# Last attention steps of a group laid over the next projection, embedding products in value banks, squares read from the bank

## Chip, core and metric

The kernel runs on one core of a Trainium2 chip. Its time is the device time of one execution in microseconds (us); lower is better. The core's engines are TensorE (PE, matmuls and transposes), VectorE (DVE), ScalarE (ACT), GpSimd (POOL) and SyncE (SP, which issues the DMAs here). Each engine runs its own instructions in order and waits for others by semaphores. Matmul results land in PSUM, which holds eight banks of 128 x 512 f32.

## What is computed

A decoder trunk of two layers, 512 tokens, width 1024. Layer 0 mixes tokens by eight stick-breaking heads and four differential heads, layer 1 by sixteen dilated heads. After each mixer come a squared-ReLU MLP and a gated per-layer embedding. The parts that matter:

```
h = h + even_mixer(hn, ...)          # layer 0;  odd_mixer in layer 1
  proj = h @ w_in;  q, k, v = split(proj)
  stick-breaking: w = sigmoid(z) * prod of later (1 - sigmoid(z)),  o = w @ v
  differential:   attn = softmax(s0) - lam * softmax(s1),  o = rmsnorm(attn @ v, subln_g) * (1 - lambda_init)
  return concat(o) @ w_out
u = square(relu(hn @ w_mlp_up));  h = h + u @ w_mlp_down
h = h + (p @ w_ple_proj) * sigmoid(rmsnorm(h) @ w_ple_gate)     # embedding products: p @ w_ple_proj
```

## The kernel before, in words

All products are made from f32 numbers split into a high and a low part (a copy on ACT, a subtraction on DVE or POOL), three matmuls each (`mm3`, lines 138, 141 and 142). Weights come in blocks by DMA and are split by `wsplit` (L122 on ACT, L126 on POOL).

A mixer has four groups of heads. In layer 0 these are two differential groups (two heads each), then two stick-breaking ones (four heads each); in layer 1 four dilated ones. `project(g)` makes the values, queries and keys of a group, 96 units of PE work in the order of the generator. `attend(...)` gives the group's steps as a list. Step n forms the scores and weights of tile n (head n // 4, query tile n % 4). It also transposes tile n - 3 and copies it into `pth` and `ptl` (L540, L541), and `combine(x)` multiplies the four tiles of a head by the values, five steps after the head's last tile. In differential groups `subnorm(x)` comes two steps later: it squares the head's output, sums over the partitions by two matmuls with `ones_r` (L622, L623) and scales by the inverse root (`rsqrt`: Ln on L210, Exp on L213, DVE on L214 to L216). Dilated and stick-breaking groups have 21 steps, differential ones 15.

`interleave(units, total, steps)` lays the steps of group n between the units of group n + 1's projection, evenly, after a lead of 8 units. All steps of a group lie within that one projection. The last group of layer 0 lies over `ple_units(1)` and `out_first`, that of layer 1 over `out_first`. The embedding products of layer 0 (`ple_units(0)`, eight of them in 512 columns) stand ahead of the last projection of the mixer, the first of them after the last differential group's steps. Each takes a bank of the pool "mm", is copied out by ACT (L365) into a tile (`tmp2` or `pjt`) and stored to DRAM.

PSUM pools have two banks each: "mm" for projections, "sc" for scores, "tp" for transposes, "pv" for combines and sub-norm sums. A bank is free again when its reader is done. `tmp2` has three buffers, which the sub-norms and the embedding products share.

The instructions' order on each engine comes from the tile framework's scheduler, which takes the program's order and the dependencies. It need not be the written order.

The built program has an instruction ACT_TABLE_LOAD on ACT wherever Sigmoid (the stick-breaking scores, L590 and L591) follows Ln or Exp (norms and softmax), and the other way round; copies and Squares stand anywhere without one.

Of the kernel before, what the change touches and what calls it, by code (L numbers as in the profile page):

```python
# [12 lines left out]
F32 = mybir.dt.float32  # L13
F32R = mybir.dt.float32r
I32 = mybir.dt.int32
AF = mybir.ActivationFunctionType
ALU = mybir.AluOpType
# [6 lines left out]
QT = S // P  # L24
# [10 lines left out]
PVLAG = 2  # L35
# [27 lines left out]
def trunk(  # L63
# [5 lines left out]
    nc = tc.nc  # L69
    uid = [0]  # L70

    def nm(s):
        uid[0] += 1
        return f"{s}_{uid[0]}"
# [15 lines left out]
    def t2k(tag, pool=None, dtype=F32):  # L90
        return (pool or (mix[0] if tag in ("tmp", "tmp2") else spool)).tile([P, S], dtype, tag=tag, name=nm(tag), bufs=T_BUFS.get(tag, 2))
# [6 lines left out]
    def ps(tag):  # L98
        return psum.tile([P, S], F32, tag=tag, name=nm(tag), bufs=PS_BUFS[tag])
# [4 lines left out]
    def ps_wide():  # L104
        t = ps(wide[wide_i[0] % 8])
        wide_i[0] += 1
        return t
# [4 lines left out]
    def wload(src):  # L112
        raw = wpool.tile([P, src.shape[-1]], F32, tag="raw", name=nm("raw"), bufs=2)
        nc.sync.dma_start(raw, src)
        return raw
# [41 lines left out]
    def run(units):  # L157
        for _ in units:
            pass

    LEAD = 8.0

    def interleave(units, total, steps):
        spent, at = -LEAD, 0
        for cost in units:
            spent += cost
            while at < len(steps) and at * (total - LEAD) < spent * len(steps):
                steps[at]()
                at += 1
        for step in steps[at:]:  # L170
            step()

    last_split = []
# [174 lines left out]
    def ple_units(layer):  # L348
        raw = wpool.tile([P, 2 * KT * P], F32, tag="raw", name=nm("raw"), bufs=2)
        nc.sync.dma_start(raw[:, 0:2 * S].rearrange("p (k c) -> p k c", k=2), pT[layer].rearrange("k p c -> p k c"))  # L350
        ph, pl = wsplit(raw, 0, 2, S)
        raw = wload(w_proj[layer])
        for c in range(2):
            wh, wl = wsplit(raw, c, 2, 512)
            for i in range(4):
                acc = ps("mm")
                sl = slice(i * P, (i + 1) * P)
                for k in range(2):
                    if layer < DEPTH - 1:
                        mm3(acc, wh[:, k, sl], wl[:, k, sl], ph[:, k], pl[:, k], k == 0, k == 1)  # L360
                    else:
                        mm3(acc, ph[:, k, sl], pl[:, k, sl], wh[:, k], wl[:, k], k == 0, k == 1)
                    yield 2.0
                t = mix[0].tile([P, S], F32, tag="bias", name=nm("pjt"), bufs=4) if i % 2 else t2k("tmp2")
                nc.scalar.activation(t, acc, AF.Copy)  # L365
                nc.sync.dma_start(pjd[layer, 4 * c + i], t)
# [5 lines left out]
    def mixer(layer, norm, nxt):  # L372
# [182 lines left out]
        def attend(g, kind, v, heads):  # L555
            LAG = 3
            nh = 2 if kind == "diff" else 4
            pts = [(pt_i[0] + x) % 2 for x in range(nh)]
            pt_i[0] += nh
            bias, ready = {}, {}  # L560

            def weights(x, i, evict):
                n = P * (i + 1)
# [34 lines left out]
            def combine(x):  # L598
                hi, lo = pth[pts[x]], ptl[pts[x]]
                if kind == "diff":  # L600
                    vh = lambda j: v[:, j, P * x:P * x + P]
                    vl = lambda j: v[:, j, 256 + P * x:256 + P * x + P]
                    op = pv([(vh, hi), (vh, lo), (vl, hi)])
                    o = oT[2 * g + x]
                    nc.scalar.activation(o, op, AF.Copy)
                    return
                vs = lambda j: v[:, j, P * x:P * x + P]
                op = pv([(vs, hi), (vs, lo)])
                a = slice(64 * (x % 2), 64 * (x % 2) + 64)
                b = slice(64 - 64 * (x % 2), 128 - 64 * (x % 2))  # L610
                o = oT[2 * g + x // 2]
                nc.scalar.activation(o[a], op[b], AF.Copy)
                nc.vector.tensor_tensor(o[a], op[a], o[a], op=ALU.add)

            def subnorm(x):
                o = oT[2 * g + x]
                hi, rs, lo = t2k("tmp2", dtype=F32R), t2k("tmp2"), t2k("tmp2", dtype=F32R)
                nc.scalar.activation(rs, o, AF.Square)
                nc.scalar.activation(hi, rs, AF.Copy)
                nc.vector.tensor_tensor(lo, rs, hi.bitcast(F32), op=ALU.subtract)  # L620
                mp = ps("pv")
                nc.tensor.matmul(mp, ones_r, hi, start=True, stop=False)  # L622
                nc.tensor.matmul(mp, ones_r, lo, start=False, stop=True)  # L623
                rsqrt(rs, t2k("tmp2"), mp, SUBLN_EPS, eps_s, scale=float(D // P))
                nc.vector.scalar_tensor_tensor(o, o, gsub, rs, op0=ALU.mult, op1=ALU.mult)

            def step(n):
                m = n - LAG
                evict = lambda: None
                if 0 <= m < QT * nh:  # L630
                    tp = transpose(ready.pop(m), m % QT)
                    evict = lambda: transposed(tp, m % QT, pts[m // QT])
                if n < QT * nh:
                    ready[n] = weights(n // QT, n % QT, evict)
                else:
                    evict()
                m = n - LAG - PVLAG
                if m >= 0 and m % QT == QT - 1 and m // QT < nh:
                    combine(m // QT)
                m -= 2  # L640
                if kind == "diff" and m >= 0 and m % QT == QT - 1 and m // QT < nh:
                    subnorm(m // QT)

            return [(lambda n=n: step(n)) for n in range(QT * nh + LAG + PVLAG + 2 * (kind == "diff"))]

        groups = GROUPS[layer]
        tiles = [2 * g + d for g in groups for d in range(2)]
# [2 lines left out]
        def spread(units, every):  # L650
            for x, cost in enumerate(units):
                if x % every == 0 and len(ohl) < 6:
                    ohl.append(split_tile(oT[tiles[len(ohl)]]))
                yield cost
# [13 lines left out]

        cur = []
        run(project(groups[0], cur))  # L670
        for n, g in enumerate(groups[1:]):
            steps = attend(*cur)
            cur = []
            if layer == 0 and n == 2:
                interleave(chain(ple_units(0), project(g, cur)), 132.0, steps)
            else:
                interleave(project(g, cur), 100.0, steps)
        if layer == 0:
            interleave(chain(spread(ple_units(1), 2), out_first()), 100.0, attend(*cur))
        else:  # L680
            interleave(out_first(), 72.0, attend(*cur))
        ohl += [split_tile(oT[k]) for k in tiles[6:8]]
        for c, (wh, wl) in enumerate(block(w_outb[layer], 2, 512)):
            for i in range(4):
                acc = ps_wide()
# [344 lines left out]
```

## Time and profile before

| what | value |
|---|---|
| median of the runs | 1310.36 us (1309.34 to 1310.42) |
| profiled execution | 1308.87 us |
| its span, first to last instruction | 1307.1 us |
| busy: PE / DVE / ACT / POOL | 1283.7 / 973.5 / 686.0 / 189.8 us |
| layer 0's mixer | about 0 to 262 us |
| layer 1's mixer | about 684 to 890 us |

The times of engines overlap, so the busy times don't add up to the span. A row of the page or of a view names a line of the kernel (L122), the engine, the tiles written and read (`wh<-raw`), and then the times. An idle time in brackets is the engine's, right before the instruction, with what released it.

### The profile page before, as it was taken

The numbers are of one execution on the slowest core, as the hardware profiler recorded it, in microseconds if no ns is written. First come the engines' busy times: TensorE is split into PE (matmuls) and PEld (weight loads), VectorE is DVE, ScalarE is ACT, GpSimd is POOL, SyncE is SP. The second block draws the span as 40 slices with busy tenths as digits, with TensorE's granted clock in tenths as the row PEclk, the third lists the DMA queues.
The fourth block names the chain that finished last, engine by engine and source line by source line (L and its number), as shares of the span: only waits on it lengthen the run. The fifth ranks groups of instructions, "written<-read, shape, count | busy, mean of one in ns | idle before, by whom it ended". The sixth has DMA issues, their size and how long they took to land.

```text
span 1307.1 us, 18561 instructions
## 1 busy us (share of the span) xinstructions
PE 1283.7 (98%) x7256; PEld 1117.4 (85%) x7256; DVE 973.5 (74%) x1623; ACT 686.0 (52%) x1117; POOL 189.8 (15%) x160
## 2 busy tenths in 40 slices
PE   9999999999999999999999999999999999999997
PEld 7988787888998989988889888788899898998876
DVE  7788888778848869845767877887784885994566
ACT  6666768554535334333456666765553443533344
POOL 2433434410000000000024333222000000000001
PEclk9999999999999999999999999999999999999999
DMA  6421423223232322323432222212223123232241
GB/s 217 135 81 50 140 93 115 89 82 112 86 108 97 102 92 97 129 97 101 157 112 96 84 89 78 69 57 95 99 97 124 70 97 129 73 122 97 97 145 65
DMA packets 28040, 133.20 MB, mean 102 GB/s; under 512 B 3312, under 2 KB 4048, under 8 KB 15280
## 3 DMA queue, kind: packets, MB, share of 16 engines
q1 hardware_dynamic: 27952, 132.01, 29.5%
q8 instruction: 57, 0.93, 0.3%
q14 instruction: 31, 0.25, 0.1%
HBM read 125.63 MB, written 6.37 MB: 101 GB/s over the span
## 4 chain that ended last, share of the span: by engine, by line
PE 85%; DVE 8%; ACT 4%; issue 1%; DMA 1%; SPq 0%; POOL 0%; ACTq 0%; DVEq 0%; POOLq 0%
PE mm L138 10%; PE mm L141 10%; PE mm L142 10%; PE sc L141 6%; PE sc L142 6%; PE sc L138 6%; PE pv L142 5%; PE pv L141 5%; PE pv L138 5%; PE tp L141 5%; PE tp L142 5%; PE tp L138 5%; PE pv L551 2%; PE tp L532 2%; PE sc L506 1%
## 5 line engine op out<-in xcount | busy, mean ns | idle before, releaser
L122 ACT ACTIVATE wh<-raw 128x1024 fp32r<-128x1024 f32 (+1 forms) x168 | 173.4, 1036 | 226.9 <-PE mm L141 63.0
L126 POOL TENSOR_TENSOR wl<-raw,wh 128x512 fp32r<-128x512 f32 (+1 forms) x132 | 177.1, 1364 | 309.3 <-ACT wh L122 303.6
L138 PE MATMUL mm<-hi,wh 128*128 128x512 f32 x472 | 187.0, 396 | 0.6 <-DVE v L443 0.4
L142 PE MATMUL mm<-hi,wl 128*128 128x512 f32 x472 | 184.8, 392 | 0.1
L141 PE MATMUL mm<-lo,wh 128*128 128x512 f32 x472 | 184.6, 391 | 0.0
L128 DVE TENSOR_TENSOR wl<-raw,wh 128x1024 fp32r<-128x1024 f32 x102 | 124.5, 1224 | 41.3 <-ACT wh L122 34.8
L142 PEld LDWEIGHTS mm<-hi,wl 128*128 128x128 f32 x472 | 88.6, 188 | 20.1 <-POOL wl L126 0.5
L138 PEld LDWEIGHTS mm<-hi,wh 128*128 128x128 f32 x472 | 88.7, 188 | 17.3 <-DVE v L443 0.6
L141 PEld LDWEIGHTS mm<-lo,wh 128*128 128x128 f32 x472 | 88.7, 188 | 15.6
L526 ACT ACTIVATE e<-e,mn 128x128 f32<-128x128 f32 (+3 forms) x96 | 53.8, 561 | 65.4 <-DVE mn L523 65.0
L754 ACT ACTIVATE wh<-raw 128x1024 fp32r<-128x1024 f32 x48 | 50.7, 1057 | 69.6 <-PE tp L141 35.1
L733 DVE TENSOR_TENSOR ul<-u,uh 128x1792 fp32r<-128x1792 f32 (+1 forms) x32 | 58.4, 1824 | 23.4 <-ACT uh L732 23.4
L732 ACT ACTIVATE uh<-u 128x1792 fp32r<-128x1792 f32 (+1 forms) x32 | 49.4, 1544 | 48.9 <-DVE u L728 48.7
L138 PE MATMUL sc<-hi,wh 128*128 128x512 f32 x184 | 71.9, 391 | 0.9 <-ACT hi L182 0.9
L141 PE MATMUL sc<-lo,wh 128*128 128x512 f32 x184 | 72.1, 392 | 0.3 <-DVE lo L183 0.3
L142 PE MATMUL sc<-hi,wl 128*128 128x512 f32 x184 | 71.8, 390 | 0.0
L721 ACT ACTIVATE u<-u 128x512 f32<-128x512 f32 x64 | 39.4, 625 | 53.8 <-DVE u L720 53.8
L142 PE MATMUL pv<-uh,wl 128*128 128x256 f32 (+1 forms) x224 | 67.4, 301 | 0.0
L142 PE MATMUL sc<-uh,wl 128*128 128x256 f32 (+1 forms) x224 | 67.3, 301 | 0.0
L141 PE MATMUL pv<-ul,wh 128*128 128x256 f32 (+1 forms) x224 | 67.2, 300 | 0.0
L141 PE MATMUL sc<-ul,wh 128*128 128x256 f32 (+1 forms) x224 | 67.2, 300 | 0.0
L138 PE MATMUL pv<-uh,wh 128*128 128x256 f32 (+1 forms) x224 | 66.6, 297 | 0.0
(259 smaller groups left out, 3645.4 us busy)
## 6 DMA issues: line engine op xcount, KB each, us to landing
raw<-in_w_up_dram SPq DMA_DIRECT2D x32, 1024.0 KB, 4.9
raw<-in_w_down_dram SPq DMA_DIRECT2D x32, 1024.0 KB, 4.9
raw<-in_w_in_dram SPq DMA_DIRECT2D x23, 1024.0 KB, 4.9
raw<-in_w_gate_dram SPq DMA_DIRECT2D x8, 1024.0 KB, 5.0
bias<-urow SPq DMA_DIRECT2D x24, 256.0 KB, 3.9
raw<-in_w_outa_dram SPq DMA_DIRECT2D x8, 768.0 KB, 4.2
pj<-pjd SPq DMA_DIRECT2D x16, 256.0 KB, 5.0
h<-in_xT_dram SPq DMA_DIRECT2D x8, 256.0 KB, 5.6
```

Of the source, the lines that this page charges most:

```text
L122: nc.scalar.activation(hi, src, AF.Copy)
L126: nc.gpsimd.tensor_tensor(lo[:, kx], src[:, kx], hi[:, kx].bitcast(F32), op=ALU.subtract)
L128: nc.vector.tensor_tensor(lo, src, hi.bitcast(F32), op=ALU.subtract)
L138: mm = nc.tensor.matmul(acc, lh, rh, start=start, stop=False)
L141: nc.tensor.matmul(acc, lh, rl, start=False, stop=False)
L142: nc.tensor.matmul(acc, ll, rh, start=False, stop=stop)
L526: nc.scalar.activation(e[:, 0:n], e[:, 0:n], AF.Exp, scale=-1.0, bias=mn, accum_out=s)
L532: nc.tensor.transpose(tp[:, j * P:(j + 1) * P], e[:, j * P:(j + 1) * P], ident)
L721: nc.scalar.activation(ui, ui, AF.Square, scale=0.5)
L732: nc.scalar.activation(uh[:, parts], u[:, parts], AF.Copy)
L733: nc.vector.tensor_tensor(ul[:, parts], u[:, parts], uh[:, parts].bitcast(F32), op=ALU.subtract)
L754: nc.scalar.activation(hi, src, AF.Copy)
```

## The change

Three edits.

1. `attend` gives two lists: the main steps (the first 4 x heads + 1, that is 17 or 9), and those left, in which only late transposes, the last combine and (in differential groups) both sub-norms happen. `interleave` takes the left ones of the group before as `tail` and lays them evenly into the first ten units (`LEAD` is 10.0, it was 8.0); the main steps follow, evenly over the other units. The last group of a layer gets its left steps behind its main ones.
2. Two of the eight embedding products, numbers 2 and 5, take a bank of "pv"; the others keep "mm".
3. Both Squares of the sub-norm (`hi` rounded, `rs` in full) are made by ACT straight from the product's bank at combine, with the copy to `o`; DVE's difference `lo` follows there. They are held until `subnorm` uses them. Before, both were made at `subnorm`, from `o`.

```diff
--- before.py
+++ after.py
@@ -158,16 +158,18 @@
         for _ in units:
             pass
 
-    LEAD = 8.0
-
-    def interleave(units, total, steps):
-        spent, at = -LEAD, 0
+    LEAD = 10.0
+
+    def interleave(units, total, steps, tail=()):
+
+        plan = [(LEAD * (x + 1) / (len(tail) + 1), step) for x, step in enumerate(tail)]
+        plan += [(LEAD + x * (total - LEAD) / len(steps), step) for x, step in enumerate(steps)]
+        spent = 0.0
         for cost in units:
             spent += cost
-            while at < len(steps) and at * (total - LEAD) < spent * len(steps):
-                steps[at]()
-                at += 1
-        for step in steps[at:]:
+            while plan and plan[0][0] < spent:
+                plan.pop(0)[1]()
+        for _, step in plan:
             step()
 
     last_split = []
@@ -353,7 +355,7 @@
         for c in range(2):
             wh, wl = wsplit(raw, c, 2, 512)
             for i in range(4):
-                acc = ps("mm")
+                acc = ps("pv" if (4 * c + i) % 3 == 2 else "mm")
                 sl = slice(i * P, (i + 1) * P)
                 for k in range(2):
                     if layer < DEPTH - 1:
@@ -557,7 +559,7 @@
             nh = 2 if kind == "diff" else 4
             pts = [(pt_i[0] + x) % 2 for x in range(nh)]
             pt_i[0] += nh
-            bias, ready = {}, {}
+            bias, ready, squares = {}, {}, {}
 
             def weights(x, i, evict):
                 n = P * (i + 1)
@@ -602,7 +604,12 @@
                     vl = lambda j: v[:, j, 256 + P * x:256 + P * x + P]
                     op = pv([(vh, hi), (vh, lo), (vl, hi)])
                     o = oT[2 * g + x]
+                    hi, rs, lo = t2k("tmp2", dtype=F32R), t2k("tmp2"), t2k("tmp2", dtype=F32R)
+                    nc.scalar.activation(rs, op, AF.Square)
+                    nc.scalar.activation(hi, op, AF.Square)
                     nc.scalar.activation(o, op, AF.Copy)
+                    nc.vector.tensor_tensor(lo, rs, hi.bitcast(F32), op=ALU.subtract)
+                    squares[x] = (rs, hi, lo)
                     return
                 vs = lambda j: v[:, j, P * x:P * x + P]
                 op = pv([(vs, hi), (vs, lo)])
@@ -614,10 +621,7 @@
 
             def subnorm(x):
                 o = oT[2 * g + x]
-                hi, rs, lo = t2k("tmp2", dtype=F32R), t2k("tmp2"), t2k("tmp2", dtype=F32R)
-                nc.scalar.activation(rs, o, AF.Square)
-                nc.scalar.activation(hi, rs, AF.Copy)
-                nc.vector.tensor_tensor(lo, rs, hi.bitcast(F32), op=ALU.subtract)
+                rs, hi, lo = squares.pop(x)
                 mp = ps("pv")
                 nc.tensor.matmul(mp, ones_r, hi, start=True, stop=False)
                 nc.tensor.matmul(mp, ones_r, lo, start=False, stop=True)
@@ -641,7 +645,8 @@
                 if kind == "diff" and m >= 0 and m % QT == QT - 1 and m // QT < nh:
                     subnorm(m // QT)
 
-            return [(lambda n=n: step(n)) for n in range(QT * nh + LAG + PVLAG + 2 * (kind == "diff"))]
+            steps = [(lambda n=n: step(n)) for n in range(QT * nh + LAG + PVLAG + 2 * (kind == "diff"))]
+            return steps[:QT * nh + 1], steps[QT * nh + 1:]
 
         groups = GROUPS[layer]
         tiles = [2 * g + d for g in groups for d in range(2)]
@@ -668,17 +673,20 @@
 
         cur = []
         run(project(groups[0], cur))
+        tail = ()
         for n, g in enumerate(groups[1:]):
-            steps = attend(*cur)
+            steps, left = attend(*cur)
             cur = []
             if layer == 0 and n == 2:
-                interleave(chain(ple_units(0), project(g, cur)), 132.0, steps)
+                interleave(chain(ple_units(0), project(g, cur)), 132.0, steps, tail)
             else:
-                interleave(project(g, cur), 100.0, steps)
+                interleave(project(g, cur), 100.0, steps, tail)
+            tail = left
+        steps, left = attend(*cur)
         if layer == 0:
-            interleave(chain(spread(ple_units(1), 2), out_first()), 100.0, attend(*cur))
+            interleave(chain(spread(ple_units(1), 2), out_first()), 100.0, steps + left, tail)
         else:
-            interleave(out_first(), 72.0, attend(*cur))
+            interleave(out_first(), 72.0, steps + left, tail)
         ohl += [split_tile(oT[k]) for k in tiles[6:8]]
         for c, (wh, wl) in enumerate(block(w_outb[layer], 2, 512)):
             for i in range(4):
```

Below, the order of the built programs, engine by engine, at the places where the prediction speaks of them. The numbers in names count buffers; they differ between the two programs.

ACT at the end of the second differential group, before: the embedding products are copied out on L365, `e` are the sigmoids, `tmp2_328` is the last sub-norm's.

```order
L122 ACTIVATE wh_355_1706<-raw_338_1639 128x1024
L213 ACTIVATE tmp2_328_1604<-tmp2_328_1604 128x512
L488 ACTIVATE kh_333_1624<-tmp_332_1622 64x512
L489 ACTIVATE kh_333_1624<-tmp_332_1622 64x512
L488 ACTIVATE kh_334_1628<-tmp_332_1622 64x512
L489 ACTIVATE kh_334_1628<-tmp_332_1622 64x512
L365 ACTIVATE tmp2_342_1653<-mm_341_1646 128x512
L365 ACTIVATE pjt_344_1663<-mm_343_1656 128x512
L590 ACT_TABLE_LOAD
L590 ACTIVATE e_347_1674<-sc_346_1670 128x128
L591 ACTIVATE e_348_1675<-sc_346_1670 128x128
```

The last sub-norm's Exp (L213) stands ahead of all sigmoids, with one table load between them. After, in the same stretch, `tmp2_340` is the last sub-norm's (Ln on L212, Exp on L215), and nine rows ahead of the first one stands another load:

```order
L367 ACTIVATE pjt_351_1693<-mm_350_1686 128x512
L122 ACTIVATE wh_376_1780<-raw_373_1776 128x1024
L212 ACT_TABLE_LOAD
L212 ACTIVATE tmp2_340_1644<-pv_344_1660,eps_s_83 128x512
L592 ACT_TABLE_LOAD
L592 ACTIVATE e_363_1739<-sc_362_1735 128x384
L215 ACT_TABLE_LOAD
L215 ACTIVATE tmp2_340_1644<-tmp2_340_1644 128x512
L593 ACT_TABLE_LOAD
L593 ACTIVATE e_364_1740<-sc_362_1735 128x384
L367 ACTIVATE tmp2_349_1683<-pv_343_1656 128x512
```

Ln and Exp now stand between the sigmoids of the first stick-breaking head, and each change between them has a load: five in this stretch, where there was one.

PE, before, where embedding product 2 begins (`mm_345`), after the scores of a stick-breaking tile:

```order
L506 MATMUL sc_351_1690<-kh_324_1560,qq_293_1411 128x256
L507 MATMUL sc_351_1690<-klz_25_183,qq_293_1411 128x256
L509 MATMUL sc_351_1690<-sbmask_90,ident_r_92 128x128
L138 MATMUL mm_345_1666<-wh_336_1634,wh_339_1641 128x512
L141 MATMUL mm_345_1666<-wl_337_1635,wh_339_1641 128x512
L142 MATMUL mm_345_1666<-wh_336_1634,wl_340_1642 128x512
L138 MATMUL mm_345_1666<-wh_336_1634,wh_339_1641 128x512
```

After, where product 5 begins (`pv_359`), in the bank that the last sub-norm's sum (`pv_344`) held:

```order
L138 MATMUL mm_361_1731<-wh_326_1581,wh_352_1696 128x512
L141 MATMUL mm_361_1731<-wl_327_1582,wh_352_1696 128x512
L142 MATMUL mm_361_1731<-wh_326_1581,wl_353_1697 128x512
L534 MATMUL tp_367_1758<-ident_72,e_347_1677 128x128
L508 MATMUL sc_368_1762<-kh_306_1489,qq_264_1332 128x512
L509 MATMUL sc_368_1762<-klz_25_183,qq_264_1332 128x512
L511 MATMUL sc_368_1762<-sbmask_90,ident_r_92 128x128
L534 MATMUL tp_378_1806<-ident_72,e_356_1709 128x128 x2
L138 MATMUL pv_359_1721<-wh_326_1581,wh_352_1696 128x512
L141 MATMUL pv_359_1721<-wl_327_1582,wh_352_1696 128x512
L142 MATMUL pv_359_1721<-wh_326_1581,wl_353_1697 128x512
```

Product 2 moved to a "pv" bank too (`pv_343`), ahead of this stretch; product 5 waits for DVE's read of `pv_344` (L217 of the new file), where before each product waited for the copies of those in the two "mm" banks.

PE in layer 1, at the end of the third dilated group's steps, before: `mm_1538` is the last key tile of the projection, `pv_1564` the last combine.

```order
L142 MATMUL mm_1538_8263<-hi_1091_6294,wl_1536_8258 128x512
L138 MATMUL mm_1538_8263<-hi_1095_6306,wh_1535_8257 128x512
L141 MATMUL mm_1538_8263<-lo_1096_6307,wh_1535_8257 128x512
L142 MATMUL mm_1538_8263<-hi_1095_6306,wl_1536_8258 128x512
L551 MATMUL pv_1564_8401<-pth_1103_6326,v_1292_7232 128x512
L551 MATMUL pv_1564_8401<-ptl_1105_6328,v_1292_7232 128x512
L551 MATMUL pv_1564_8401<-pth_1103_6326,v_1292_7232 128x384
L551 MATMUL pv_1564_8401<-ptl_1105_6328,v_1292_7232 128x384
```

After, `mm_1570` and `mm_1571` are the first products of `out_first`, `tp` the last two transposes, `pv_1580` the last combine:

```order
L534 MATMUL tp_1574_8422<-ident_72,e_1552_8334 128x128 x3
L138 MATMUL mm_1570_8410<-hi_1575_8428,wh_1566_8400 128x512
L141 MATMUL mm_1570_8410<-lo_1576_8429,wh_1566_8400 128x512
L142 MATMUL mm_1570_8410<-hi_1575_8428,wl_1567_8401 128x512
L534 MATMUL tp_1577_8435<-ident_72,e_1558_8355 128x128 x4
L138 MATMUL mm_1571_8411<-hi_1575_8428,wh_1568_8405 128x512
L141 MATMUL mm_1571_8411<-lo_1576_8429,wh_1568_8405 128x512
L142 MATMUL mm_1571_8411<-hi_1575_8428,wl_1569_8406 128x512
L138 MATMUL mm_1570_8410<-hi_1578_8445,wh_1566_8400 128x512
L141 MATMUL mm_1570_8410<-lo_1579_8446,wh_1566_8400 128x512
L142 MATMUL mm_1570_8410<-hi_1578_8445,wl_1567_8401 128x512
L553 MATMUL pv_1580_8452<-pth_1103_6326,v_1289_7208 128x512
```

The last transposes moved from the projection's end to behind the next block's first matmuls, and the combine lies between that block's products.

## Rows read from the trace of the kernel before

**Rows 1.** the page, part 1: busy us (share of the span) and instructions.
```profile
PE 1283.7 (98%) x7256; PEld 1117.4 (85%) x7256; DVE 973.5 (74%) x1623; ACT 686.0 (52%) x1117; POOL 189.8 (15%) x160
```

**Rows 2.** windows of core 0: length, busy us (instructions) by engine, PEclk, DMA.
```profile
80.00:100.00 20.00, 17.16 (x100) 14.53 (x99) 15.66 (x23) 12.57 (x22) 7.43 (x5) 1.00 0.15 53
120.00:160.00 40.00, 37.46 (x195) 31.07 (x194) 32.70 (x44) 31.80 (x59) 17.68 (x13) 1.00 0.38 126
160.00:200.00 40.00, 40.00 (x246) 35.44 (x245) 36.05 (x51) 25.74 (x53) 15.17 (x12) 1.00 0.28 93
200.00:240.00 40.00, 38.25 (x198) 31.48 (x197) 33.53 (x49) 30.26 (x65) 16.62 (x13) 1.00 0.29 101
700.00:900.00 200.00, 196.96 (x1135) 169.32 (x1135) 152.21 (x408) 131.81 (x296) 66.83 (x52) 1.00 0.25 84
```

**Rows 3.** waits of PE, waiting line <- releaser: us in all, times, longest.
```profile
PE mm L138 <- ACT tmp L365: 2.5, 2, 1.4
PE pv L622 <- ACT tmp L619: 2.4, 2, 1.2
...
PE sc L506 <- DVE mn L523: 1.4, 2, 1.0
PE pv L551 <- ACT pth L540: 1.3, 1, 1.3
```

**Rows 4.** timeline of PE around 139.7 us: start, duration, what, idle before.
```profile
137.92 0.39 PE L141 MATMUL mm<-lo,wh 128*128 128x512 f32 x1
138.15 0.39 PE L142 MATMUL mm<-hi,wl 128*128 128x512 f32 x1
139.74 0.49 PE L622 MATMUL pv<-tmp,ones_r 128*128 128x512 f32 x1 [1.21 <-ACT tmp L619]
140.47 0.50 PE L623 MATMUL pv<-tmp,ones_r 128*128 128x512 f32 x1 [0.23 <-DVE tmp L620]
140.81 0.40 PE L138 MATMUL mm<-hi,wh 128*128 128x512 f32 x1
```

**Rows 5.** timeline of ACT around two table loads, at 146.6 and 632.4.
```profile
146.01 0.58 ACT L365 ACTIVATE pjt<-mm 128x512 f32<-128x512 f32 x1
146.61 1.28 ACT L590 ACT_TABLE_LOAD   x1
147.91 0.28 ACT L590 ACTIVATE e<-sc 128x128 f32<-128x128 f32 x1
...
632.38 1.28 ACT L842 ACT_TABLE_LOAD   x1
635.38 1.23 ACT L842 ACTIVATE gt<-gt 128x512 f32<-128x512 f32 x2 [1.71 <-DVE gt L841]
```

**Rows 6.** groups by line and shape, 60 to 260 us: busy, mean ns.
```profile
L122 ACT ACTIVATE wh<-raw 128x1024 fp32r<-128x1024 f32 x21 | 22.2, 1055 | 2.7 <-PE mm L141 1.8 <-PE mm L142 0.5 <-issue 0.3
...
L488 ACT ACTIVATE kh<-tmp 64x512 fp32r<-64x512 f32 x12 | 7.5, 627 | 6.1 <-DVE tmp L474 6.0
L540 ACT ACTIVATE pth<-tp 128x512 fp32r<-128x512 f32 x12 | 7.1, 593 | 6.1 <-PE tp L532 6.0
...
L210 ACT ACTIVATE tmp<-pv,eps_s 128x512 f32<-128x512 f32 x4 | 2.8, 690 | 2.7 <-PE pv L623 2.6
L618 ACT ACTIVATE tmp<-o 128x512 f32<-128x512 f32 x4 | 2.5, 632 | 0.1
...
L213 ACT ACTIVATE tmp<-tmp 128x512 f32<-128x512 f32 x4 | 2.5, 627 | 0.1
...
L605 ACT ACTIVATE o<-pv 128x512 f32<-128x512 f32 x4 | 2.3, 576 | 0.0
...
L214 DVE TENSOR_TENSOR tmp<-tmp 128x512 f32<-128x512 f32 x4 | 4.1, 1025 | 1.6 <-ACT tmp L213 1.6
...
L215 DVE SCALAR_TENSOR_TENSOR tmp<-pv,tmp 128x512 f32<-128x512 f32 x4 | 2.7, 683 | 0.1
```

**Rows 7.** DMA issues, 130 to 160 us: KB each, us to landing.
```profile
pjd<-tmp SPq DMA_DIRECT2D x4, 256.0 KB, 4.3
```

## The prediction

> **What bounds the kernel now.** I read the page first. TensorE (PE) is busy 1283.7 us of a span of 1307.1 [rows 1]. Only time in which PE stands still can be won, so the next view is the table of windows over the two mixers, the part that the change touches; PE's clock is granted in full (1.00) in each of them. Between the changes of group PE is busy for the whole stretch, as at 160 to 200. The idle time sits where one group ends and the next begins [rows 2]: 2.84 us at 80 to 100 (diff to diff, which I call T1), 2.54 at 120 to 160 (diff to stick-breaking, T2), 1.75 at 200 to 240 (stick-breaking to output projection, T3), and 3.04 in layer 1 at 700 to 900. The waits of PE name the causes [rows 3]: sub-norm squares (L619), evacuations of embedding products (L365), scores' minima (L523) and late copies of transposes (L540); the others are shorter.
>
> An idle time is not yet a loss. At T2 the matmul that starts at 139.74 follows a start at 138.15, 1.59 us for a step that took 0.23 just before, so an idle time of 1.21 costs 1.36. The second stalled product then takes 0.34 to the next start [rows 4], 0.11 more than 0.23. I charge 0.26 for each stall beside its idle time. With four stalls at T1 (the two sums' products and two of scores), three at T2, two at T3 and about eight in layer 1, the removable losses are 2.84 + 1.04 = 3.9, 2.54 + 0.78 = 3.3, 1.75 + 0.52 = 2.3 and 3.04 + 2.08 = 5.1: **14.6 us**. That is all the change can reach; the MLPs keep PE full and are untouched.
>
> **Spreading the last steps.** Before, the transposes of the last tiles, the last combine and both sub-norms follow each other within the last part of the next group's projection, and the last combine comes directly after its copies. Now they lie two units (sb and dil groups) or 1.4 units (diff groups) apart in the first ten units of the following projection. The work is the same. In layer 1 the product of the last head no longer follows the projection's end, and matmuls of the next block lie between transposes, copies and product. What still waits there, by hand: the last copy (0.59) [rows 6] partly behind two splits, 0.3 to 0.4 at each of three places, and a few refills. 5.1 becomes 1.2, **-3.9**. At the bounds, nothing waits (-5.1), or each place keeps 0.8 (-2.5). I take the value near the first, since ScalarE (ACT) is far from full there.
>
> At T1 the sub-norm products have matmuls ahead of them, and the minima no longer queue behind them. New is that PE comes early: the copy for combine(1) stands on ACT behind the four copies of a key tile, 4 x 0.63 [rows 6], and PE waits about 1.1 for it; the two sub-norm products and an evacuation leave 0.5. 3.9 becomes 1.6, **-2.3** (bounds -0.5 and -3.9). At T3 the same copy costs 0.5 and two embedding evacuations 0.8: 2.3 becomes 1.3, **-1.0** (0 to -2.3).
>
> **Squares from PSUM.** Four times, ACT did a copy, a Square and a copy (0.58 + 0.63 + 0.63) [rows 6]; now two Squares and a copy, all from the bank. No row shows a Square from a bank; between the copy's 0.58 and the other Square's 0.63 the sum is 1.74 to 1.89, against 1.84. I take no change of time on ACT. The split is ready a copy earlier, which is in the terms above. The price: the three buffers of a tile are held from combine to sub-norm, and the embedding products share this pool. The second sub-norm's difference (VectorE, DVE) must wait for the store of an embedding tile, 4.3 us after its issue [rows 7]; behind that difference stand the second sum product, its Ln and its Exp.
>
> **Embedding products in value banks.** Products 2 and 5 use the banks of the combines and sub-norms, the other six alternate on two. That takes away the waits of 1.10 at T2 and 1.44 at T3 on L365 [rows 3]; but product 5 now waits in PE's order until DVE has read the second sub-norm's bank (L215, L217 in the new file), and everything behind it on PE waits too.
>
> **T2, where it turns.** The order shows what the diff doesn't: ACT loads tables five times here, once before. The Ln and Exp of the last sub-norm now stand between sigmoids of the first stick-breaking scores, and the two need different tables. A load takes 1.28, and 1.30 pass from its start to the next instruction [rows 5]. If a wait would have stood there anyway the price could fall towards nothing; the longest row is 2.99, from 632.38 to 635.38, though that idle time is put down to DVE. I take 1.30.
>
> Then I add up ACT's order from combine(0)'s product. Its first Square can start 2.25 us after the product's first matmul (three products of 512, three of 384 and six of 256 columns, and 0.3 to the first reader). Up to the Exp of the second sub-norm it has four loads (5.2), two splits (2.1), four key copies (2.5), two transposes' copies (1.1), six squares and copies (3.7), two Ln and two Exp (2.6), three embedding evacuations (0.5 from start to start, 1.5) and five short sigmoids (1.5), all but the evacuations and sigmoids by [rows 5, 6]: 20.2. ACT never waits long in it, so the Exp ends at 22.5. DVE's two instructions follow (L214 0.68 to 1.37, mean 1.03; L215 0.68) [rows 6], and product 5 may start at about 24.2. PE's own work up to there is 54 products of 512 columns at 0.23 (12.4), 8 of 384 and 16 of 256 columns in proportion (3.2), ten transposes and four masks at 0.1 (1.4): 17.0. So PE stands still for 7.2, in portions (about 1.1 at the copy for combine(1), 0.5 at product 2, some at the sums, the most at product 5), and hardly at all after: 7.2 in place of 3.3, **+3.9**. With DVE at its shortest, and evacuations and copies overlapping by 0.1 each, it is 5.5; with the store landing late, another 1.4: 8.6. So +2.2 to +5.3.
>
> The Trainium skill, page "ScalarE: Activation LUTs", section "What ACT_TABLE_LOAD costs", gives 1283 ns for the load and about 1380 ns of drain ahead of it, 2.66 us for each switch. The load's duration agrees with the trace; the drain does not show, since the load at 146.61 starts where the evacuation before it ends [rows 5]. By the page's figure the sum would be 5.4 us higher.
>
> **The sum.** -3.9 - 2.3 - 1.0 + 3.9 = -3.3. The profiled execution took 1308.87 us (span 1307.1 and 1.8 around it) and would take 1305.6. It is 1.5 below the median of the runs, so against the median of 1310.36 I forecast **1307.1 us**. About 0.2%, 2.6 us, is what a measurement of this kernel can tell from no change, so the forecast lies just beyond it.
>
> **Rivals.** (1) T2's chain is hidden: the loads fall into ACT's waits, or evacuations run into each other, and PE reaches product 5 when its bank is free. Then T2 keeps about 2.5 and the sum is -8.0: 1302.4 us. For it speaks that instructions on ACT start before their predecessor ends; against it, that ACT is busy 31.80 of 40 us there already [rows 2]. Chance 0.17.
> (2) The stalls only move: at each change of group PE now reaches the product early and waits for a copy behind others on ACT. Five places at 1.3 to 1.6 and T2 at 7.2 make 14.0 of 14.6: 1309.8 us. For it speaks the queue of four key copies, against it that in layer 1 these lie further off. Chance 0.17.
> (3) A switch of tables costs more than its row. The place is T2, the price by the longest row 4 x (2.99 - 1.30) = 6.8 more: +3.5, **1313.9 us**, slower. It decides once T2 loses over 13.1, a price of 2.8 a switch. Against it stands the load at 146.61, followed after 1.30 [rows 5]. Chance 0.10, with a T2 chain that is longer for another reason in it.
> (4) ACT empties itself ahead of each switch, at a price between the two rows, 1.30 and 2.99. In the middle that is 0.85 more for each of four loads, 3.4 in all, and the sum is +0.1: 1310.5 us, no change. Chance 0.06. This is what the page of the Trainium skill states; with its figure the time would be 1312.5, also within 0.2%.
> The forecast itself: 0.50, with 1304.8 to 1309.6 as its own range.
>
> **How the numbers follow.** Faster by over 0.2% (under 1307.7): 0.31 of the forecast's half, rival 1 and a little of rival 2, 0.50. Within 0.2%: the rest of the forecast, most of rival 2, rival 4, 0.40. Slower: 0.10. A range of 1302.5 to 1312.5 leaves out rival 3 and about half of rival 1, 0.18.
>
> **What would show it.** Five loads in T2, four of them between the second sub-norm's and the sigmoids' instructions, each 1.28 and 1.30 to the next start; a PE wait of several us at an embedding product in a value bank, released by L217 of the new file (L215 before); the windows of T1 and layer 1 near 20.00. No long wait at that product would make rival 1 right, and waits for pth of over 1 us at each change rival 2. If the idle time in layer 1 stays at 3 us, the spreading failed.

## The result and the profile after

The changed kernel takes 1315.84 us (median of five runs, 1315.10 to 1316.63) against 1309.73 before (five runs, 1308.74 to 1310.42; the median of 1310.36 that the forecast started from is that of the first three). The ratio is 1.0047, 95% interval 1.0032 to 1.0062: **slower**, by about 6 us. Faster was forecast, 1307.1 us in a range of 1302.5 to 1312.5. The profiled execution took 1316.63 us with a span of 1314.9, 7.8 more than before.

The page's line of busy times, to [rows 1]: PE is busy 4.4 us longer for the same 7256 matmuls.

```profile
PE 1288.1 (98%) x7256; PEld 1121.6 (85%) x7256; DVE 970.8 (74%) x1623; ACT 688.9 (52%) x1121; POOL 190.4 (14%) x160
```

The windows, to [rows 2] (columns as there):

```profile
80.00:100.00 20.00, 18.98 (x126) 17.20 (x125) 15.93 (x30) 15.74 (x32) 5.76 (x5) 1.00 0.23 80
120.00:160.00 40.00, 35.16 (x162) 28.60 (x161) 30.00 (x58) 34.38 (x64) 11.88 (x8) 0.92 0.30 110
...
200.00:240.00 40.00, 36.60 (x184) 30.16 (x183) 31.95 (x48) 28.81 (x63) 11.50 (x10) 0.96 0.28 93
700.00:900.00 200.00, 196.32 (x1160) 170.37 (x1159) 159.87 (x408) 134.83 (x301) 67.95 (x52) 1.00 0.25 80
```

PE's idle time in these windows fell at 80 to 100 (2.84 to 1.02) and rose in the others: 2.54 to 4.84 at T2, 1.75 to 3.40 at T3, 3.04 to 3.68 in layer 1. In two of the windows the granted clock is no longer 1.00. The waits of PE, to [rows 3]:

```profile
PE pv L553 <- ACT pth L542: 4.1, 5, 1.2
PE pv L138 <- DVE tmp L217: 4.1, 1, 4.1
PE mm L138 <- ACT pjt L367: 2.0, 1, 2.0
...
PE mm L138 <- DVE tmp L476: 1.4, 1, 1.4
```

The waits for squares (L619 before) and for evacuations at T2 are gone. New are one wait of 4.1 us for the sub-norm's bank, five for late copies (there was one), and two at T3 (2.0 and 1.4).

For a sum by place I take, for each matmul, the time to the next start and subtract what a product of that width takes undisturbed (0.23 us for 512 columns, 0.12 for 256). The excess, summed over a stretch, holds idle time, refilling and slow clock:

| lost, us | T1 (70 to 112) | T2 (112 to 178) | T3 (178 to 262) | layer 1 (684 to 900) |
|---|---|---|---|---|
| before | 4.7 | 5.6 | 6.0 | 11.4 |
| after | 2.8 | 11.0 | 9.3 | 12.2 |
| difference | -1.9 | +5.4 | +3.3 | +0.8 |
| predicted | -2.3 | +3.9 | -1.0 | -3.9 |

The losses depend on what the narrow products are charged, their differences only by about 0.3 us. The differences sum to 7.6 of the 7.8 us.

**T2.** ACT's timeline (start, duration, what) shows the chain of loads as the order had it:

```profile
149.60 1.28 ACT L592 ACT_TABLE_LOAD   x1
150.89 0.49 ACT L592 ACTIVATE e<-sc 128x384 f32<-128x384 f32 x1
151.40 1.28 ACT L215 ACT_TABLE_LOAD   x1
152.69 0.63 ACT L215 ACTIVATE tmp<-tmp 128x512 f32<-128x512 f32 x1
153.34 1.28 ACT L593 ACT_TABLE_LOAD   x1
154.63 0.49 ACT L593 ACTIVATE e<-sc 128x384 f32<-128x384 f32 x1
```

Each load takes 1.28 us, and 1.29 to 1.30 pass to the next start, as in [rows 5]; the first two of the five stand at 141.89 and 147.60. PE's timeline beside it (idle time before in brackets):

```profile
150.31 0.39 PE L534 MATMUL tp<-ident,e 128*128 128x128 f32 x2
154.83 0.80 PE L138 MATMUL pv<-wh,wh 128*128 128x512 f32 x1 [4.13 <-DVE tmp L217]
155.42 0.63 PE L141 MATMUL pv<-wl,wh 128*128 128x512 f32 x1
155.85 0.63 PE L142 MATMUL pv<-wh,wl 128*128 128x512 f32 x1
```

Product 5 starts at 154.83, after 4.1 us in which PE has nothing else to do. Behind it the steps take 0.43 us from start to start where they took 0.23. The windows there:

```profile
150.00:155.00 5.00, 0.87 (x6) 0.57 (x5) 1.58 (x3) 4.93 (x6) 0.20 (x1) 0.83 0.00 0
155.00:160.00 5.00, 5.00 (x12) 3.94 (x13) 4.72 (x8) 3.52 (x10) 0.00 (x0) 0.50 0.53 200
160.00:165.00 5.00, 5.00 (x42) 4.91 (x42) 1.37 (x2) 2.92 (x5) 3.88 (x3) 0.99 0.26 77
```

The granted clock is at half (1.2 in place of 2.4 GHz) for the five microseconds after the idle time, and back at full by 160. Twelve products at 0.43 in place of 0.23 are 2.4 us on top of the wait.

**Layer 1.** At the first change of group there, ACT and then PE:

```profile
751.58 0.62 ACT L490 ACTIVATE kh<-tmp 64x512 fp32r<-64x512 f32 x1
752.22 0.59 ACT L619 ACTIVATE o<-pv 64x512 f32<-64x512 f32 x1
752.84 0.63 ACT L491 ACTIVATE kh<-tmp 64x512 fp32r<-64x512 f32 x1
753.49 0.63 ACT L490 ACTIVATE kh<-tmp 64x512 fp32r<-64x512 f32 x1
754.14 0.63 ACT L491 ACTIVATE kh<-tmp 64x512 fp32r<-64x512 f32 x1
754.79 0.98 ACT L542 ACTIVATE pth<-tp 128x384 fp32r<-128x384 f32 x2
```

```profile
751.55 0.49 PE L534 MATMUL tp<-ident,e 128*128 128x128 f32 x3
...
752.60 0.60 PE L534 MATMUL tp<-ident,e 128*128 128x128 f32 x4
...
755.82 0.50 PE L553 MATMUL pv<-pth,v 128*128 128x512 f32 x1 [1.20 <-ACT pth L542]
```

The last transposes start at 751.55 and 752.60, but four copies of a key tile (L490, L491, 2.5 us) and an output copy stand ahead of their two copies, which start at 754.79. PE has passed its units by 754.6 and waits 1.20. The second change of group looks the same (1.19), the third keeps 0.5.

**T3.** PE's second wait there, and ACT:

```profile
225.25 0.42 PE L508 MATMUL sc<-kh,qq 128*128 128x384 f32 x1
227.66 0.50 PE L138 MATMUL mm<-hi,wh 128*128 128x512 f32 x1 [2.00 <-ACT pjt L367]
...
229.51 0.63 PE L141 MATMUL mm<-lo,wh 128*128 128x512 f32 x1
229.94 0.63 PE L142 MATMUL mm<-hi,wl 128*128 128x512 f32 x1
```

```profile
226.74 0.38 ACT L593 ACTIVATE e<-sc 128x256 f32<-128x256 f32 x1 [1.79 <-DVE e L597]
227.02 0.59 ACT L367 ACTIVATE pjt<-mm 128x512 f32<-128x512 f32 x1
```

An embedding's copy (L367) stands on ACT behind a sigmoid that waited for DVE (that idle time of ACT, 1.79 us, is put down to L597, which frees its buffer). PE waits 2.0 us for the copy, and from 229.0 to 231.6 its steps take 0.43 again. The first wait there, 1.4 us at 209.7, is for a bank that DVE's scaled copy L476 reads; on DVE two splits (L182) and L620 stand directly ahead of that copy.

### The profile page after: what moved, and what is told of

Same layout as the page of the kernel before. It is cut to its first block, busy times and chain, and to the rows that moved or that the text cites. A ratio compares the mean times of both kernels' runs of the same rounds, so it can differ in the third digit from the quotient of the medians.

```text
span 1314.9 us, 18575 instructions
## 1 busy us (share of the span) xinstructions
PE 1288.1 (98%) x7256; PEld 1121.6 (85%) x7256; DVE 970.8 (74%) x1623; ACT 688.9 (52%) x1121; POOL 190.4 (14%) x160
## 4 chain that ended last, share of the span: by engine, by line
PE 81%; DVE 10%; ACT 5%; issue 2%; DMA 1%; SPq 0%; POOL 0%; ACTq 0%; DVEq 0%
PE mm L138 10%; PE mm L141 10%; PE mm L142 10%; PE sc L141 6%; PE sc L142 6%; PE sc L138 5%; PE pv L142 5%; PE pv L141 5%; PE pv L138 5%; PE tp L141 5%; PE tp L142 5%; PE tp L138 5%; PE pv L553 2%; DVE qq L483 1%; PE tp L534 1%
```

## Experiments

Two theories stood after the result. **S**: the spreading costs, since it puts the last sub-norm between sigmoids (tables) and the last copies behind those of a key tile. **B**: the value banks cost, since a product now waits for a sub-norm's bank. Each kernel was timed beside the kernel before, on the same chip; before had medians of 1309.4 to 1309.8 us in these. Diffs are against the changed kernel unless another is named.

**No spreading.**

```diff
-    LEAD = 10.0
+    LEAD = 8.0
...
             steps, left = attend(*cur)
+            steps, left = steps + left, []
...
-            tail = left
+            tail = ()
```

> The changed kernel with the first edit undone: every step of a group lies in the next projection again and the lead is 8 units; value banks and squares from the bank stay. Theory S (the loss comes from the spreading: the last sub-norm's Ln and Exp fall between sigmoids, and copies of the last transposes fall behind copies of a key tile): one table load around 147 us instead of five, no wait over 1.5 us, full clock, and the gains of the two other edits alone, 1306 to 1309 us. Theory B (the value banks cost: a product waits for the sub-norm's bank): the wait of PE for L217 (or its like) stays at 2 us or more, and the time is 1312 us or more.

1305.82 us, 0.9974 of before (0.9964 to 0.9983): faster than before, and a little under the expected range. At T2 there is one table load, and no wait of PE at the changes of group is over 1.3 us. This is the unspread kernel of the runs below. The two other edits win 3.6 us, and the spreading with its lead costs 10.0. B falls.

```profile
80.00:100.00 20.00, 17.99 (x108) 15.44 (x107) 16.33 (x27) 12.75 (x25) 7.08 (x5) 1.00 0.15 54
120.00:160.00 40.00, 39.41 (x214) 33.35 (x214) 34.49 (x45) 31.28 (x60) 19.46 (x13) 1.00 0.42 135
200.00:240.00 40.00, 39.30 (x207) 32.47 (x207) 33.82 (x51) 28.71 (x65) 16.43 (x12) 1.00 0.32 112
700.00:900.00 200.00, 197.17 (x1116) 169.41 (x1115) 153.06 (x406) 132.70 (x295) 64.20 (x50) 0.99 0.24 80
```

Against [rows 2], T1, T2 and T3 have 0.8, 2.0 and 1.1 us less idle time; layer 1's is as before, but a stretch at half clock (842.8 to 845.8) follows a wait of 1.28 us there.

**No value banks.**

```diff
-                acc = ps("pv" if (4 * c + i) % 3 == 2 else "mm")
+                acc = ps("mm")
```

> The changed kernel with the second edit undone: all eight embedding products take banks of the pool mm. Theory S: ACT's order keeps its four extra loads between sigmoids, Ln and Exp, so products wait for evacuations that stand behind these loads instead of for L217; the stall of PE around 150 us stays between 2.5 and 5 us, the clock falls again behind it, 1313 to 1317 us. Theory B: the wait around 150 us falls under 1.5 us and the time under 1311 us.

1314.38 us, 1.0041 (1.0028 to 1.0053). The loss at T2 stays and only changes its name, as S had it:

```profile
PE sc L508 <- ACT e L593: 2.4, 1, 2.4
PE mm L138 <- ACT tmp L367: 2.0, 1, 2.0
```

Scores wait for a sigmoid behind the loads (2.4 us), then a product for an evacuation (2.0), and the granted clock is 0.50 from 152 to 158.

**Squares from the output again.** The squares and the difference return to `subnorm`, as before the change.

> The changed kernel with the third edit undone: the squares are made at the sub-norm from the copied output again. Theory S: the chain at 150 us gets longer by one to two operations of 0.6 us on ACT, and T1 too: 1316 to 1319 us. If the three buffers held from combine to sub-norm were a cause of the loss, the time falls to 1314 us or less.

1317.49 us, 1.0061 (1.0049 to 1.0074), 1.7 over the changed kernel. The wait for L217 is 4.6 us where it was 4.1, so the squares from the bank look like a gain here too; the two intervals overlap, which leaves it likely and not shown. The held buffers don't show as a cause of the loss here; with one table load they do, below.

**The last differential group whole.**

```diff
             steps, left = attend(*cur)
+            if layer == 0 and n == 1:
+                steps, left = steps + left, []
```

> The changed kernel, except that the last differential group's steps all lie in the next projection, as before the change; the other groups stay spread. Theory S: one table load instead of five at that place, no wait of 4 us there and full clock in the window 140 to 160, which is 5 to 7 us less than the changed kernel: 1309 to 1311 us; layer 1 and the place around 220 us stay as they are. Theory B: product 5 still waits for a sub-norm's bank by over 2 us, 1313 us or more.

1309.13 us, 0.9995 (0.9986 to 1.0004), 6.7 under the changed kernel. T2 loses 2.4 us in all (11.0 after).

```profile
120.00:160.00 40.00, 39.83 (x230) 34.93 (x228) 31.70 (x43) 31.05 (x58) 19.86 (x13) 1.00 0.43 141
...
700.00:900.00 200.00, 196.01 (x1115) 168.77 (x1115) 157.15 (x403) 130.13 (x293) 66.46 (x52) 0.99 0.24 80
```

So T2's tail costs 8.6 us at its place, and 6.7 of kernel time here. Most of the gap is layer 1: in this profile it loses about 1.8 us more than in the changed kernel, with a stretch at half clock (748 to 751) behind a wait of 1.24 us.

**One table load, all spread.** An ordering edge: the first sigmoid comes after the last sub-norm's Exp.

```diff
+                if last_exp and not sig_tail:
+                    order(s0.ins, last_exp[0])
```

> The changed kernel with one ordering edge more: the first sigmoid of the stick-breaking groups comes after the last sub-norm's Exp. All steps stay spread, value banks and squares stay; the program has one table load in that stretch and not five. Theory S (the alternating tables make the chain that product 5 waits for): the wait for the sub-norm's bank falls from 4.1 to under 1.5 us, the clock in the window 140 to 160 stays at 1.00, and the time is 1308 to 1311 us, as with the steps left whole (1309.1). If spreading alone makes the chain too long, with or without loads, the wait stays over 3 us and the time over 1313 us.

1311.86 us, 1.0019 (1.0010 to 1.0027): between the two expectations. The alternating loads cost 4.0 us of kernel time, clock included (1.00 at 140 to 160 now); at T2 itself the loss falls from 11.0 to 7.9. The wait for the bank is down to 0.3, and another came up; PE's waits, then DVE's timeline:

```profile
PE pv L630 <- DVE tmp L614: 2.3, 1, 2.3
```

```profile
146.22 1.41 DVE L614 TENSOR_TENSOR tmp<-tmp,tmp 128x512 fp32r<-128x512 f32 x1 [2.55 <-DMA pjd<-tmp]
```

The second sum's product waits 2.3 us for the difference L614, and that for the store of an embedding tile, whose buffer of `tmp2` it needs.

**The embedding tiles in their own pool**, on top of the last:

```diff
-                t = mix[0].tile([P, S], F32, tag="bias", name=nm("pjt"), bufs=4) if i % 2 else t2k("tmp2")
+                t = mix[0].tile([P, S], F32, tag="bias", name=nm("pjt"), bufs=4) if i % 2 or not layer else t2k("tmp2")
```

> The spread kernel with one table load (1311.9 us), and the embedding products of layer 0 copied into tiles of their own pool, so that the squares no longer wait for the store of such a tile. Theory H (the squares, held from combine to sub-norm in three buffers that the embedding products share, cost the 2.3 us that are left at the second sum's product): that wait falls under 0.8 us and the time to 1308.5 to 1310 us, what the kernel with this place unspread takes (1309.1). If the stall only moves on to a bank, the time stays over 1311 us.

1310.02 us, 1.0002 (0.9993 to 1.0011): 1.8 us less, the wait for L614 is gone, and T2's excess falls from 7.9 to 5.4. Squares held in shared buffers were the second part. Spread, T2 still loses 3.0 us more at its place than whole (2.4), and the kernel is 0.9 slower: spreading T2 gains nothing even so.

**Squares alone.** The kernel before with the third edit as its only one.

> The kernel before with the squares from the bank as its only edit (no spreading, all embedding products in the pool mm). The two waits for the sub-norm's square (1.2 us each) fall to 0.4 and the waits for embedding evacuations (1.1 and 1.4) stay: 1.5 to 2 us faster than before, 1307.5 to 1308.3 us; the value banks then give the rest of the 3.6 us of the unspread kernel. If the squares were all of its gain: 1305.8 us.

1308.23 us, 0.9991 (0.9982 to 1.0000): 1.4 us faster, inside the expected 1307.5 to 1308.3 and at the edge of what can be told. The value banks give the other 2.4 of the unspread kernel.

**T1 alone spread**, lead 10:

```diff
+            if layer or n:
+                steps, left = steps + left, []
```

> The changed kernel with one place spread, the tail of the first differential group (T1); all other groups lie whole in the next projection, at a lead of 10. Theory S: T2 with one table load and no wait over 0.5 us, the place at 220 us with 0.5 at most and full clock, layer 1 as in the kernel before (3 us idle). 1304 to 1306 us. If spreading had no part in the waits of layer 1 and at 220 us, these stay and the time is 1308 us or more.

1302.82 us, 0.9948 (0.9936 to 0.9960): **7.0 us faster than before, the lowest median here**, and below the 1304 to 1306 expected. Its windows, beside [rows 2]:

```profile
120.00:160.00 40.00, 39.82 (x227) 34.86 (x226) 33.61 (x46) 31.89 (x61) 19.16 (x12) 1.00 0.43 145
200.00:240.00 40.00, 39.64 (x210) 33.08 (x210) 35.22 (x53) 29.07 (x67) 17.93 (x14) 1.00 0.32 112
700.00:900.00 200.00, 196.63 (x1109) 167.75 (x1108) 158.51 (x404) 132.36 (x294) 63.48 (x49) 1.00 0.24 80
```

**The lead alone.** The unspread kernel with a lead of 10.

> The unspread kernel (1305.8 us) with one number changed, the lead of 10 units for 8; no tail anywhere. If the 3.0 us between it and the kernel with T1 alone spread come from the tail at T1, it stays at 1305 to 1306.5 us. If they come from the later and wider placed steps, it reaches 1302.5 to 1304 us, and the spread of T1 gives less than 1 us.

1304.16 us, 0.9958 (0.9946 to 0.9971), between the two expectations. Of the 3.0 us from the unspread kernel to T1 alone, 1.7 come from the lead. The rest isn't won at T1: there the two lose 2.9 (lead) and 3.3 us (tail). It lies ahead of it, where the lead alone has a wait of 1.1 us at 59.9 (for L445, the low part of values) that the kernel with T1 spread does not have. The two intervals overlap, so whether the tail at T1 wins anything stays open.

**T1 and T3.** As T1 alone, with `if layer or n == 1`.

> The kernel with T1 alone spread (1302.8 us) plus one more spread place: the tail of the first stick-breaking group, over the embedding products of layer 1 (T3). Theory S: two waits come back there, 1.4 us for a query's or key's scaled copy on DVE and 2.0 for an embedding product's bank, with a stretch at half clock behind: 3 to 4.5 us slower, 1306 to 1307.3 us. If the loss at that place came from T2 being spread as well, the time stays at 1302 to 1304 us.

1306.68 us, 0.9976 (0.9966 to 0.9986): 3.9 slower than T1 alone, with both waits (1.4 and 2.0) back and T3's excess at 9.0 (4.1 without).

**T1 and layer 1.** As T1 alone, with `if not layer and n`.

> The kernel with T1 alone spread (1302.8 us) plus the spreading in layer 1. Theory S: the last combine's waits for copies come back there (1.2, 1.5 and 0.5 us), 0 to 2 us slower, 1303 to 1305 us; the sum with the run before it explains the kernel that spreads all but T2 (1309.1). By the prediction's term (layer 1 wins 3.9 us) it would be 1299 us.

1303.37 us, 0.9952 (0.9939 to 0.9964). The waits on the copies are back (1.2, 1.2, 0.5); the time differs from T1 alone by 0.55, less than the intervals tell apart. No 3.9 us are won. The expectation also said that this run and the one before it explain the kernel that spreads all but T2. They don't quite: 1302.82 + 3.9 + 0.55 is 1307.2, and that kernel takes 1309.1; its stretch at half clock in layer 1, which this run does not have, fits the gap.

**Twenty units**, on top of the kernel with T2 whole: `LEAD = 20.0`.

> The kernel with the last differential group's steps whole (as the run before it), and the tail of the other groups laid over 20 units of the next projection, not 10. Theory Q (in layer 1 the last copies stand on ACT behind the four copies of a key tile, 2.6 us, and ten units of 0.36 us are too short for them): the three waits of the last combine for its copy (1.2 to 1.5 us each) fall under 0.4, layer 1 wins 2.5 to 3.5 us, 1305 to 1307 us in all. Rival P (the scheduler sets the last combine right behind its copies wherever the step is written): the three waits stay over 1 us and the time stays at 1308 to 1310 us.

1310.89 us, 1.0005 (0.9996 to 1.0014). The waits on `pth` in layer 1 are gone, so the distance was what lacked there (Q). The time still did not fall, against Q's 1305 to 1307; others took their place, among them:

```profile
PE tp L534 <- DVE r L585: 2.9, 4, 0.8
```

**Half of the key copies on DVE.**

```diff
-                        nc.scalar.activation(kh[b], f[a], AF.Copy)
+                        nc.vector.tensor_copy(kh[b], f[a])
```

> The changed kernel, spreading and all, with every second copy of a key tile made by DVE and not by ACT (24 times two copies of about 0.63 us leave ACT). Theory Q: the last combines of layer 1 wait 1.0 to 1.3 us less for their copies (sum of the waits on pth from 4.1 to under 1.5 us), layer 1 wins 2 to 3.5 us; the place at 150 us wins up to 1.3 us of its chain. 1310 to 1313 us. If ACT's queue isn't what the combines wait for, the waits on pth stay over 3 us and the time at 1314 us or more.

1326.72 us, 1.0133 (1.0120 to 1.0146). A miss: the waits on `pth` nearly vanish, but DVE now makes the low part of each transposed tile too late, for longer.

```profile
PE pv L553 <- DVE ptl L543: 6.9, 4, 1.9
```

**A deliberate stall** in the unspread kernel: six copies of a tile onto itself ahead of embedding product 5.

```diff
+                if layer == 0 and c == 1 and i == 1:
+                    for _ in range(6):
+                        nc.scalar.activation(ph[:, 0], ph[:, 0].bitcast(F32), AF.Copy)
```

> The unspread kernel (1305.8 us) with one deliberate stall: at the sixth embedding product ACT copies a tile onto itself six times, and PE's next product reads it; the result is the same. Six copies of 0.5 to 0.63 us give PE an idle time of 3 to 4.5 us. Theory K (a long idle time costs a stretch at half clock behind it): the granted clock of the window behind it falls to half for some us, and the time rises by the idle time and 1.5 to 2.5 us more, 1310 to 1313 us. Without such a price the time rises by the idle time alone and the clock stays at 1.00.

1312.74 us, 1.0022 (1.0014 to 1.0031), 6.9 over the unspread kernel.

```profile
148.00:152.00 4.00, 2.74 (x15) 1.89 (x13) 2.76 (x6) 3.98 (x11) 0.00 (x0) 1.00 0.97 328
152.00:156.00 4.00, 2.06 (x9) 1.53 (x10) 3.00 (x6) 4.00 (x10) 0.00 (x0) 0.93 0.38 145
156.00:158.00 2.00, 2.00 (x6) 1.51 (x6) 1.97 (x4) 0.95 (x3) 1.64 (x2) 0.50 0.00 0
158.00:160.00 2.00, 2.00 (x9) 1.59 (x8) 1.32 (x3) 1.17 (x4) 0.93 (x1) 0.79 0.36 135
```

PE is idle for 3.2 us of the eight from 148 to 156, in pieces of 1.2 us at most, and the two windows behind are at 0.50 and 0.79. In the stretch 112 to 178 it loses 5.5 us more than unstalled: the idle time, the refilling of each piece and seven products at half clock (1.4). K holds in kind: idle time made on purpose brings the half clock. A single long idle time was not what this run made.

## Why the prediction was wrong

The sum of -3.3 came as +7.6 by place. Of the 10.9 between them, layer 1 has 4.7, T3 4.3, T2 1.5 and T1 0.4.

**T1, -2.3: -1.9.** The step held in the main: the squares no longer wait, and the late copy for combine(1) costs 0.6 us of idle time and its low part 0.4, where the sum had 1.1 for the copy and 0.5 for other waits. The net agrees better than its terms. The waits for minima went from 1.4 us in two to 0.8 in one, not to nothing, and that one lies at 118 and counts under T2.

**T2, +3.9: +5.4.** The mechanism was the one forecast: five loads, 1.30 each, and product 5 waiting for DVE's L217. The chain from the product's first matmul (131.81) to product 5 took 23.0 us where the sum said 24.2. So the step on the chain was right to a twentieth. With the sum's 17.0 us of work for PE that leaves 6.0 in place of 7.2, 4.1 of it in the one wait. What failed is the words "and hardly at all after": the prediction had no term for the clock behind a long idle time (2.4 us). Another 1.0 is the wait for a score's minimum at 118. The prediction read 1.00 in every window of before and didn't ask what a wait nearly three times as long as any there would do. The wait for a store that it named does not show in the changed kernel, where DVE is idle for 0.17 us ahead of that difference; it came up (2.3 us) when the loads went.

**Layer 1, -3.9: +0.8.** The largest error. The step that failed is the last copy "partly behind two splits, 0.3 to 0.4 at each of three places". At two of the three, four key copies stand ahead, as at T1, where the same text had counted them, and PE waits 1.2 us there. Behind that is a unit taken for a time: a tail step comes two units later than the last, and a unit of the value products is 0.36 us, so 0.7 us of products lie between steps. Before, steps lay 4.4 units of 0.34 us apart, 1.5 us. The traces agree: the last two groups of transposes start 1.05 us apart (751.55 and 752.60) where it was 1.72, and PE has 1.9 us of work from the last of them to the combine where it had 3.2. The change that was to spread the last steps packed them closer. Rival 2, that the stalls only move, describes this place. PE before, at the same change of group:

```profile
740.01 0.49 PE L532 MATMUL tp<-ident,e 128*128 128x128 f32 x3
...
741.73 0.60 PE L532 MATMUL tp<-ident,e 128*128 128x128 f32 x4
...
744.92 0.39 PE L551 MATMUL pv<-pth,v 128*128 128x512 f32 x1
```

**T3, -1.0: +3.3.** The step that failed is "the same copy costs 0.5 and two embedding evacuations 0.8". No late copy shows there; in its place stands the wait of 1.4 for L476 on DVE, which the sum did not have. One evacuation costs 2.0 and not 0.8 for two, with a stretch of 2.6 us at half clock behind it. The sum sized them by ACT's own work and missed that a sigmoid ahead of the evacuation waits for DVE (1.79 us, by the trace's releaser). That this place alone costs 3.9 us is shown by T1 and T3 against T1 alone; the links of the chain are read from the trace, not tested one by one.

**The other edits.** "I take no change of time on ACT" fits: two Squares and a copy from the bank take 0.60, 0.60 and 0.61 us on average in layer 0, 1.81 against 1.84. The gain of the squares alone is 1.4 us, and that of the banks, forecast as waits of 1.1 and 1.4, is 2.4.

Rival 3 came nearest in time (1313.9), by a price of table loads that no load here had: each of the five began 0.02 us after the end of the instruction ahead of it, and the next one started 1.29 to 1.30 us after the load's start. The drain that the Trainium skill counts with each switch, on the page "ScalarE: Activation LUTs", section "What ACT_TABLE_LOAD costs", therefore shows neither ahead of a load nor behind it; the page does not say on which side it lies, the prediction put it ahead.

## What to carry to other kernels

Laying work out over another stage is worth what the distance is in time, not in steps: compute the microseconds between a copy's producer and its reader, and what stands ahead of it on its engine. Where two stages use different function tables on ACT, keep one's last use ahead of the other's first; an ordering edge did it here for 4 us. When an edit bundle loses, its parts may still win: without the spreading of three of four places, the same bundle is 7.0 us faster than before.

## What was not expected of the hardware

After some waits of PE, a stretch at half clock (0.50, 1.2 GHz) followed, 2.5 to 5.4 us long: after 4.1 us at T2 and 2.0 us at T3 in the changed kernel, and after 3.2 us in pieces in the stalled one. The length of the wait alone does not decide it. In the kernel without value banks a wait of 2.0 us at T3 left the clock at 1.00, and so did 2.3 us at T2 and 2.0 us at T3 with one table load. Two waits of 1.3 and 0.5 us in layer 1 were followed by half clock in the unspread kernel (0.99 over 700 to 900) and not in before, where they were the same. What decides between these was not tried.
